# Sample tokens' hi and lo parts as one 128-column stationary operand in a streaming encoder layer

## The chip, the cores and the metric

The kernel runs on one core of a Trainium2 chip. The metric is the device time of one execution in microseconds (us), here the median of three runs. A profiled execution gives a trace of every instruction on TensorE (matmul, PE; its weight loads, PEld), VectorE (DVE), ScalarE (ACT), GpSimd (POOL) and SyncE (SP), and of every DMA.

## What is computed

One step of a one-layer streaming encoder on 2048 prompt tokens and 64 sample tokens, 1024 channels, all in 32-bit floats. Both groups of tokens go through the same layer with the same weights; only their conditioning vectors, their convolution history and their attention keys differ.

```
h  = rms_norm(x) * (1 + sc1) + sh1
z  = h @ w_in                      # conv pair | q | k | v | two gates
u  = glu_a * sigmoid(glu_b)        # causal depthwise conv, LayerNorm, swish, projection
o  = band_attention(q, k, v)       # own chunk of 64 and 8 chunks before, per-head bias
m  = sigmoid(g_conv) * conv_out + sigmoid(g_attn) * attn_out
x  = x + gt1 * (m @ w_o)
h2 = rms_norm(x) * (1 + sc2) + sh2
x  = x + gt2 * ((silu(gate) * up) @ w_ffn_out)   # gate, up = h2 @ w_ffn_in, 2816 each
```

Outputs are the two results and the new convolution, key and value states.

## The kernel before, in words

**Three passes per product.** Each operand of a large product is kept as two parts in a matmul format: hi, a copy that ScalarE makes (`split`, L706), and lo, what is left, which VectorE or POOL subtracts. A product is the sum of three passes (`mm3`, L700): hi x hi, hi x lo and lo x hi; lo x lo is left out. Each pass is one LDWEIGHTS of the stationary operand and one MATMUL that streams the other one, up to 512 columns.

**Two forms.** In *column form* the weights are stationary and tokens stream (convolution pair, gates, merge, FFN up). In *row form* a tile of tokens is stationary, up to 128 of them as columns, and 512 weight columns stream; the result has tokens on the partitions of a PSUM bank. Row form serves q, k and v (`qkv`, L1168, and `first_block`, L899), the output projection (`wo`, L1836) and the FFN's down products (`add_down`, L2136; later blocks also `down_pair` and `add_last`).

**Token tiles.** `token_tiles` (L65) makes the 64 sample tokens a tile of their own, ahead of 128-token prompt tiles. So only the first token block of each phase, tokens 0 to 575 (`PBLOCKS`, `CBLOCKS`), has a sample tile, and in row form its stationary operand has 64 columns.

**Order of the work.** The first phase goes through four token blocks: q, two convolution channels, k, one more step of convolution, v, and so on, gates, with attention and convolution taps let in between. The second phase goes through three blocks: merge, output projection with residual and norm, turn into columns, FFN. What is let in between is decided while the program is written: `Stream` (L170) keeps an estimated clock for each engine, every instruction adds its estimated time, and the lanes (`norm_lane`, `work`, `attn`, `conv`, `tail`, `turns`) issue their next step when TensorE's clock has come far enough. `spend` (L207) ticks that clock after each `mm3`. Weights come from memory through staging tiles, are split by ScalarE and VectorE or POOL (`Weights.split`, L451), and are freed as products are done.

**Places that the change touches.** `turn` (L926) makes the columns of the first block from transposes: VectorE scales them, ScalarE writes `hh`, VectorE writes `hl`. `product` in `first_block` (L955) and in `qkv` (L1173) runs the passes for q, k and v; `qk_rows` and `v_rows` take the finished bank. `merge` (L1677) writes the merged columns as `m[0]` (hi) and `m[1]` (lo). `residual` (L1710) multiplies the projection's banks by the gate, adds x, norms, and transposes. `hidden` (L1900) writes the FFN's hidden columns to `hid` as hi and lo, in two halves of 288 tokens in the first block. `add_down` adds a pair of hidden rows' products for each token tile to an accumulator `acc`; the first pair is copied there by ScalarE, later ones are added by VectorE, and the last group goes through gate and residual to the output. PSUM has four banks (`gp`) for these products in the second phase, two per token tile.

Of the kernel before, what the change touches and what calls it, by code (L numbers as in the profile page):

```python
# [8 lines left out]
F32 = mybir.dt.float32  # L9
# [7 lines left out]
P = 128  # L17
# [594 lines left out]
def streaming_layer(ctx: ExitStack, tc: tile.TileContext, I, O):  # L612
# [87 lines left out]
    def mm3(ps, lh, ll, rh, rl, first, last, **kw):  # L700
# [2 lines left out]
        pe.matmul(ps, ll, rh, start=False, stop=last, **kw)  # L703
        stream.spend()

    def split(hi, lo, src):  # L706
        act.activation(hi, src, AF.Copy)
        stream.after("dve", "act")
        dve.tensor_tensor(lo, src, hi.bitcast(F32), ALU.subtract)
# [49 lines left out]
    def temp(name, shape=(P, 512)):  # L759
        return wk.tile(list(shape), F32, tag="t", name=name, bufs=NT)  # L760
# [138 lines left out]
    def first_block(xs):  # L899

        tiles = token_tiles(*PBLOCKS[0])
        vectors, taps, begun = setup()
        taps = taps()

        def scale_rows(a, b):
            for x_t, (t, n) in list(zip(xs, tiles))[a:b]:
                r = square(x_t, n)
                dve.tensor_scalar(x_t[:n], x_t[:n], r, None, ALU.mult)

        def modulation(ct):  # L910
# [12 lines left out]

            return rest

        def turn(k):  # L926
            pt = ps_a.tile([P, 2, 512], F32, tag="s", name="pt")
            for i, (t, n) in enumerate(tiles):
                o = pt[:, 0, t : t + n] if i < 4 else pt[:, 1, :n]
                pe.transpose(o, xs[i][:n, k * P : (k + 1) * P], ident[:n, :n])  # L930
            h = wk.tile([P, QB + SMP], F32, tag="pr", name="h32", bufs=8)
            for a, e, o, w in ((0, SMP, pt[:, 0, :SMP], 1), (SMP, 448, pt[:, 0, SMP:448], 0), (448, 576, pt[:, 1, :P], 0)):
                dve.tensor_scalar(h[:, a:e], o, A1[:, k, w : w + 1], B1[:, k, w : w + 1], ALU.mult, ALU.add)

            for c in (slice(0, 448), slice(448, 576)) if not k else (slice(0, 576),):
                split(hh[:, k, c], hl[:, k, c], h[:, c])


        with tc.issue_after(begun[0]), tc.issue_after(begun[1]):
            scale_rows(0, 2)  # L940
            rest = modulation(0)
            vectors()
            rest()
            sums_turned = pe.last.ins
            with tc.issue_after(dve.last.ins):
                scale_rows(2, 5)
            with tc.issue_after(act.last.ins), tc.issue_after(dve.last.ins):
                W.reach = W.held
                W.fill()
        with tc.issue_after(sums_turned):  # L950
            turn(0)
        pss = [ps_g.tile([P, 512], F32, tag="gp", name="ps") for _ in tiles]
        ws = {}

        def product(i, k):  # L955
            t, n = tiles[i]
            if k // 2 not in ws:
                ws[k // 2] = W.get(("qkv", 0, k // 2))
            wh, wl = ws[k // 2]
            mm3(pss[i][:n], hh[:, k, t : t + n], hl[:, k, t : t + n], wh[:, k % 2], wl[:, k % 2], k == 0, k == KT - 1)  # L960
            if i == len(tiles) - 1 and k % 2:
                W.done()

        for k in range(KT - 2):
            if k == 2:
                with tc.issue_after(act.last.ins):
                    next(taps)
            turn(k + 1)
            if k and k % 2 == 0:
                rest = modulation(k + 2)  # L970
            for i in range(len(tiles)):
                if i == 2 and not k:
# [167 lines left out]
    def norm_tile(lo, t, free):  # L1140

        c = slice(t - lo, t - lo + P)
        while t not in ahead_x:
            load_ahead()
        x_t, landed = ahead_x.pop(t)
        yield landed
        r = square(x_t, P)
        yield stream.when("pool")
        dve.tensor_scalar(x_t, x_t, r, None, ALU.mult)
        yield stream.when("dve") + PE_LAG  # L1150
        for g in range(2):
# [12 lines left out]
            f = slice(4 * g, 4 * g + 4)  # L1164
            act.activation(hh[:, f, c], h, AF.Copy)
            yield stream.when("act")
            dve.tensor_tensor(hl[:, f, c], h, hh[:, f, c].bitcast(F32), ALU.subtract)
    def qkv(b, m, norms):  # L1168
        lo, hi = PBLOCKS[b]
        tiles = token_tiles(lo, hi)  # L1170
# [2 lines left out]
        def product(t, n, ps, k):  # L1173
            if k // 2 not in ws:
                ws[k // 2] = W.get(("qkv", m, k // 2))
            wh, wl = ws[k // 2]
            c = slice(t - lo, t - lo + n)
            mm3(ps[:n], hh[:, k, c], hl[:, k, c], wh[:, k % 2], wl[:, k % 2], k == 0, k == KT - 1)
            if (t, n) == tiles[-1] and k % 2:
                W.done()  # L1180

        for t, n in tiles:
# [2 lines left out]
            ps = ps_g.tile([P, 512], F32, tag="gp", name="ps")  # L1185
            for k in range(KT):
                product(t, n, ps, k)
            if m == 0:
                work.start(qk_rows(ps, n, gqk[:, 0:1], q_d, t, None))
            elif m == 1:  # L1190
# [485 lines left out]

    def merge(c0, c1, src, m, ahead, load):  # L1677
        n = c1 - c0
        for ct in range(KT):
            g = ahead.pop(0)  # L1680
            if ct == 2 and load:
# [28 lines left out]
    def residual(pp, t, n, gt1, a, half, hs, free, last, i):  # L1710
# [91 lines left out]
    for s, (lo, hi) in enumerate(CBLOCKS):  # L1802
# [4 lines left out]
        for i, (c0, c1) in enumerate(chunks):  # L1807
# [28 lines left out]
            def wo(i, k):  # L1836
# [2 lines left out]
                    ws[k] = W.get(("wo", k))  # L1839
                wh, wl = ws[k]  # L1840
                c = slice(t - c0, t - c0 + n)
                for j in range(2):
                    f = slice(512 * j, 512 * j + 512)
                    mm3(pp[j][:n], m[0][:, k, c], m[1][:, k, c], wh[:, 0, f], wl[:, 0, f], k == 0, k == KT - 1)
                if i == len(grp) - 1:
                    W.done()

# [50 lines left out]
            return hid[i][:, f % 2]  # L1898

        def hidden(f, i, ps):  # L1900
            hi, lo = (hid_of(f)[:, j, i * half : (i + 1) * half] for j in range(2))
            stream.after("act", "dve")
            split(hi, lo, ps)

        class Operands:

# [229 lines left out]
        def add_down(fs, ws):  # L2136

            last = fs[-1] == NF - 1
            for i, (t, n) in enumerate(tiles):
# [6 lines left out]
                for e, j in [(e, j) for e in fs for j in range(2)] if last and not i else [(e, j) for j in range(2) for e in fs]:  # L2146
                    h = hid_of(e)
                    f = slice(512 * j, 512 * j + 512)
                    w = ws[e - fs[0]]
                    mm3(pss[j][:n], h[:, 0, c], h[:, 1, c], w[0][:, 0, f], w[1][:, 0, f], e == fs[0], e == fs[-1])  # L2150
                for j, ps in enumerate(pss):
                    f = slice(512 * j, 512 * j + 512)
                    dst = acc[i][:n, f]
                    stream.after("dve", "pe")
                    if fs[0] == 0:
                        act.activation(dst, ps[:n], AF.Copy)
                    elif not last:
                        dve.tensor_tensor(dst, dst, ps[:n], ALU.add)
# [96 lines left out]
```

## Time and profile before

| | |
|---|---|
| median of 3 runs | 2991.47 us (2991.17 to 2992.53) |
| profiled execution, first to last instruction (span) | 2988.4 us |
| median less span | 3.1 us |
| mean granted TensorE clock | 0.993 |
| TensorE busy | 97% of the span, 16259 matmuls |
| weight loads busy | 87% |
| VectorE, ScalarE, POOL busy | 68%, 45%, 38% |
| moved by DMA | 628 MB, 210 GB/s |

The profile gives of its own execution the span alone; what lies around it is taken as the 3.1 us by which the median of the runs is longer. Busy times of TensorE overlap, since a matmul starts while the one before it drains; the distance between starts is the better measure of a pass. In a row of groups stand the engine, the operation, output and inputs by name, the shape (stationary rows * columns, then the streamed shape), the count, then busy time and the mean length of one in ns, then idle time before them and what ended it.

### The profile page before, as it was taken

To read this page: it belongs to the slowest core of one execution; us is meant where nothing else is said; L and a number is where in the kernel's file an instruction comes from. 1 tells how busy PE (TensorE), PEld (TensorE's weight loads), DVE (VectorE), ACT (ScalarE), POOL (GpSimd) and SP (SyncE) were. 2 spreads that over 40 slices of the span, in tenths; PEclk is the share of its full clock that TensorE was granted. 3 is DMA by queue.
4 is the path that set the end of the run, shared out by engine and by line. 5 is a ranking of instruction groups with operands and counts; after the bars stand their busy time and mean duration, and the time that the engine had idled before them with its cause. 6 is when DMAs were issued, how large, how long until landed. Compare 5 with 4: busy or idle time off the path is not lost. (4 is left out here: it accounts for less than half of the span.)

```text
span 2988.4 us, 44911 instructions
## 1 busy us (share of the span) xinstructions
PE 2911.8 (97%) x16259; PEld 2594.0 (87%) x16259; DVE 2025.1 (68%) x3596; ACT 1355.2 (45%) x2437; POOL 1140.8 (38%) x734
## 2 busy tenths in 40 slices
PE   7999899999999999989999999999999999999999
PEld 4899777787888788878989899999999999999998
DVE  5897687668857885477777755666666657466666
ACT  3345643661465257464444335534444345344442
POOL 0201310111011102444666443255766741465667
PEclk9999999999999999999999999999999999999999
DMA  9989889978987888885444786323333975233333
GB/s 307 305 289 299 271 288 304 280 254 276 304 272 222 278 253 277 267 280 167 139 148 151 231 266 223 132 90 113 113 106 115 307 245 183 95 96 115 115 103 127
DMA packets 467725, 628.06 MB, mean 210 GB/s; under 512 B 36277, under 2 KB 314665, under 8 KB 467502
## 3 DMA queue, kind: packets, MB, share of 16 engines
q1 hardware_dynamic: 453456, 605.58, 62.7%
q10 hardware_dynamic: 14045, 19.60, 1.9%
q8 instruction: 128, 2.10, 0.3%
q14 instruction: 96, 0.78, 0.1%
HBM read 476.53 MB, written 148.54 MB: 209 GB/s over the span
## 5 line engine op out<-in xcount | busy, mean ns | idle before, releaser
L102 PE MATMUL ps<-t,whi 128*128 128x384 f32 (+1 forms) x2112 | 502.6, 322 | 10.3 <-ACT t L102 4.9
L102 POOL TENSOR_TENSOR wlo<-wst,whi 128x1024 fp32r<-128x1024 f32 (+1 forms) x157 | 357.8, 2289 | 288.6 <-ACT whi L102 256.3
L102 ACT ACTIVATE whi<-wst 128x1024 fp32r<-128x1024 f32 (+1 forms) x264 | 257.4, 977 | 335.6 <-PE ps L102 115.9
L102 PE MATMUL ps<-b,whi 128*128 128x384 f32 (+1 forms) x1584 | 381.4, 326 | 6.1 <-DVE early L102 3.3
L102 PEld LDWEIGHTS ps<-t,whi 128*128 128x128 f32 x2112 | 367.5, 188 | 17.8 <-ACT t L102 5.1
L102 DVE SCALAR_TENSOR_TENSOR y<-u,wd,y 128x512 f32<-128x512 f32 (+1 forms) x480 | 369.1, 773 | 6.3
L102 PE MATMUL ps<-hh,whi 128*128 128x512 f32 (+2 forms) x992 | 361.6, 365 | 0.0
L102 DVE TENSOR_TENSOR acc<-acc,pd 128x512 f32<-128x512 f32 (+1 forms) x464 | 311.6, 685 | 67.5 <-PE pd L102 64.8
L102 PE MATMUL ps<-hl,whi 128*128 128x512 f32 (+2 forms) x992 | 345.6, 348 | 0.0
L102 PE MATMUL ps<-hh,wlo 128*128 128x512 f32 (+2 forms) x992 | 345.1, 348 | 0.0
L102 PE MATMUL ps<-t,wlo 128*128 128x384 f32 (+1 forms) x1056 | 339.3, 321 | 1.0 <-POOL wlo L102 0.7
L102 PE MATMUL pd<-whi,hid 128*128 128x512 f32 (+1 forms) x1016 | 325.0, 391 | 0.0
L102 PEld LDWEIGHTS ps<-b,whi 128*128 128x128 f32 x1584 | 278.5, 189 | 12.0 <-DVE early L102 4.2
L102 POOL TENSOR_TENSOR r<-t,mhalf 128x1 f32<-128x1 f32 (+3 forms) x68 | 83.6, 1231 | 455.8 <-DVE t L102 450.6
L102 PE MATMUL ps<-b,wlo 128*128 128x384 f32 (+1 forms) x792 | 256.9, 325 | 0.0
L102 ACT ACTIVATE pr<-pr,sm 128x640 f32<-128x640 f32 (+3 forms) x272 | 200.2, 747 | 109.0 <-DVE sm L102 106.3
L102 PEld LDWEIGHTS pd<-whi,hid 128*128 128x128 f32 (+1 forms) x1016 | 185.9, 183 | 44.5 <-ACT hid L102 0.7
L102 PEld LDWEIGHTS ps<-hh,wlo 128*128 128x128 f32 x992 | 186.7, 188 | 21.8
L102 PEld LDWEIGHTS ps<-hh,whi 128*128 128x128 f32 x992 | 187.2, 189 | 18.6 <-issue 1.6
L102 PEld LDWEIGHTS ps<-hl,whi 128*128 128x128 f32 x992 | 187.5, 189 | 15.6 <-issue 1.4
L102 PEld LDWEIGHTS ps<-t,wlo 128*128 128x128 f32 x1056 | 198.2, 188 | 2.5 <-POOL wlo L102 1.3
L102 PE MATMUL pd<-wlo,hid 128*128 128x512 f32 (+1 forms) x508 | 198.4, 391 | 0.0
(225 smaller groups left out, 6174.2 us busy)
## 6 DMA issues: line engine op xcount, KB each, us to landing
whi<-w_din_h SPq DMA_DIRECT2D x72, 512.0 KB, 6.9
wlo<-w_din_l SPq DMA_DIRECT2D x72, 512.0 KB, 8.5
wst<-sum_d SPq DMA_DIRECT2D x132, 256.0 KB, 2.7
wfo<-in_w_ffn_out SPq DMA_DIRECT2D x64, 512.0 KB, 3.4
wmod<-in_w_ada SPq DMA_DIRECT2D x46, 512.0 KB, 6.2
sum_d<-ws SPq DMA_DIRECT2D x88, 256.0 KB, 3.2
wst<-in_w_ffn_in SPq DMA_DIRECT2D x84, 256.0 KB, 3.1
wst<-in_w_in SPq DMA_DIRECT2D x40, 512.0 KB, 8.5
```

Source lines behind the costliest of these rows:

```text
L102: self.last = f(*args, **kw)
```

## The change

For the sample tile the hi and the lo part stand side by side as one stationary operand of 128 columns, lo in columns 0 to 63 and hi in columns 64 to 127. Two passes, with the weights' hi and then lo part streaming, put the lo rows' product on partitions 0 to 63 of the bank and the hi rows' on 64 to 127 (`mm2`). Afterwards `fold` copies the upper half of the bank to a tile on ScalarE and adds it to the lower half on VectorE. The product lo x lo, left out before, is now part of the sum.

For q, k and v a new tile `both` (in the buffers of tag `vv`, which the attention's values use later) is filled by POOL with copies of the sample columns of `hl` and `hh`. For the output projection and the down products of the first block, `merge` and `hidden` write the parts where they belong: hi is moved up by 64 columns, and the sample's lo columns go in front of it, by a subtraction of their own. The accumulators of `add_down` hold all 128 partitions, and the fold comes once, in the last group. Column-form products, prompt tiles and the later FFN blocks keep three passes.

```diff
+    def mm2(ps, both, rh, rl, first, last, **kw):
+        pe.matmul(ps, both, rh, start=first, stop=False, **kw)
+        pe.matmul(ps, both, rl, start=False, stop=last, **kw)
+        stream.spend()
+
+    def fold(ps, t):
+        stream.after("act", "pe")
+        act.activation(t, ps[SMP : 2 * SMP], AF.Copy)
+        stream.after("dve", "act")
+        dve.tensor_tensor(ps[:SMP], ps[:SMP], t, ALU.add)
...
@@ turn @@
+            for j, x in enumerate((hl, hh)):
+                stream.after("pool", "dve")
+                gps.tensor_copy(both[:, k, SMP * j : SMP * j + SMP], x[:, k, :SMP].bitcast(F32))
...
@@ first_block and qkv @@
+            if t < SMP:
+                fold(pss[i], temp("fold")[:n])
             work.start(qk_rows(pss[i], n, gqk[:, 0:1], q_d, t, None, i > 2))
...
+    both = wk.tile([P, KT, P], F32R, tag="vv", name="both", bufs=2)
+
+    def rows_product(ps, t, n, k, wh, wl, lo):
+        c = slice(t - lo, t - lo + n)
+        if t < SMP:
+            mm2(ps, both[:, k], wh, wl, k == 0, k == KT - 1)
+        else:
+            mm3(ps[:n], hh[:, k, c], hl[:, k, c], wh, wl, k == 0, k == KT - 1)
...
@@ merge (cut is SMP for the chunk with the sample tokens, else 0) @@
-            split(m[0][:, ct, :n], m[1][:, ct, :n], ps[1])
+            hi = m[0][:, ct, cut : cut + n]
+            act.activation(hi, ps[1], AF.Copy)
+            stream.after("dve", "act")
+            if cut:
+                dve.tensor_tensor(m[0][:, ct, :cut], ps[1][:, :cut], hi[:, :cut].bitcast(F32), ALU.subtract)
+            dve.tensor_tensor(m[1][:, ct, cut:n], ps[1][:, cut:], hi[:, cut:].bitcast(F32), ALU.subtract)
...
@@ residual @@
+            if t < SMP:
+                fold(pp[j], x1[:n, f])
             stream.after("dve", "pe")
             dve.tensor_tensor(pp[j][:n], pp[j][:n], gt1[which][:n, f], ALU.mult)
...
@@ wo @@
+                    if t < SMP:
+                        mm2(pp[j], m[0][:, k, : 2 * SMP], wh[:, 0, f], wl[:, 0, f], k == 0, k == KT - 1)
+                    else:
+                        mm3(pp[j][:n], a[:, c], m[1][:, k, c], wh[:, 0, f], wl[:, 0, f], k == 0, k == KT - 1)
...
@@ hidden, first block only @@
+            hi = h[:, 0, SMP:][:, c]
+            act.activation(hi, ps, AF.Copy)
+            stream.after("dve", "act")
+            cut = 0 if i else SMP
+            if cut:
+                dve.tensor_tensor(h[:, 0, :cut], ps[:, :cut], hi[:, :cut].bitcast(F32), ALU.subtract)
+            dve.tensor_tensor(h[:, 1, c][:, cut:], ps[:, cut:], hi[:, cut:].bitcast(F32), ALU.subtract)
...
@@ add_down @@
+                    if t < SMP:
+                        mm2(pss[j], h[:, 0, : 2 * SMP], w[0][:, 0, f], w[1][:, 0, f], e == fs[0], e == fs[-1])
...
-                    dst = acc[i][:n, f]
+                    dst = acc[i][:, f]
...
-                        dve.tensor_tensor(ps[:n], ps[:n], dst, ALU.add)
+                        dve.tensor_tensor(ps, ps, dst, ALU.add)
+                        dst = dst[:n]
+                        if t < SMP:
+                            fold(ps, dst)
                         dve.tensor_tensor(ps[:n], ps[:n], gt[:n, f], ALU.mult)
```

More of the change, by code (lines that the diff above doesn't have):

```diff
@@ L959, in product @@
             wh, wl = ws[k // 2]
-            mm3(pss[i][:n], hh[:, k, t : t + n], hl[:, k, t : t + n], wh[:, k % 2], wl[:, k % 2], k == 0, k == KT - 1)
+            rows_product(pss[i], t, n, k, wh[:, k % 2], wl[:, k % 2], 0)
             if i == len(tiles) - 1 and k % 2:
@@ L1176, in product @@
             wh, wl = ws[k // 2]
-            c = slice(t - lo, t - lo + n)
-            mm3(ps[:n], hh[:, k, c], hl[:, k, c], wh[:, k % 2], wl[:, k % 2], k == 0, k == KT - 1)
+            rows_product(ps, t, n, k, wh[:, k % 2], wl[:, k % 2], lo)
             if (t, n) == tiles[-1] and k % 2:
@@ L1187, in qkv @@
                 product(t, n, ps, k)
+            if t < SMP:
+                fold(ps, temp("fold")[:n])
             if m == 0:
@@ L1678, in merge @@
         n = c1 - c0
+        cut = 0 if c0 else SMP
         for ct in range(KT):
@@ L1841, in wo @@
                 c = slice(t - c0, t - c0 + n)
+                a = m[0][:, k, 0 if c0 else SMP :]
                 for j in range(2):
                     f = slice(512 * j, 512 * j + 512)
-                    mm3(pp[j][:n], m[0][:, k, c], m[1][:, k, c], wh[:, 0, f], wl[:, 0, f], k == 0, k == KT - 1)
+                    if t < SMP:
+                        mm2(pp[j], m[0][:, k, : 2 * SMP], wh[:, 0, f], wl[:, 0, f], k == 0, k == KT - 1)
+                    else:
+                        mm3(pp[j][:n], a[:, c], m[1][:, k, c], wh[:, 0, f], wl[:, 0, f], k == 0, k == KT - 1)
                 if i == len(grp) - 1:
@@ L1900, in hidden @@
         def hidden(f, i, ps):
-            hi, lo = (hid_of(f)[:, j, i * half : (i + 1) * half] for j in range(2))
+            h = hid_of(f)
+            c = slice(i * half, (i + 1) * half)
             stream.after("act", "dve")
-            split(hi, lo, ps)
+            if s:
+                split(h[:, 0, c], h[:, 1, c], ps)
+                return
+            hi = h[:, 0, SMP:][:, c]
[5 more added lines that the diff above has]
+            dve.tensor_tensor(h[:, 1, c][:, cut:], ps[:, cut:], hi[:, cut:].bitcast(F32), ALU.subtract)
         class Operands:
@@ L2149, in add_down @@
                     w = ws[e - fs[0]]
-                    mm3(pss[j][:n], h[:, 0, c], h[:, 1, c], w[0][:, 0, f], w[1][:, 0, f], e == fs[0], e == fs[-1])
+                    if t < SMP:
+                        mm2(pss[j], h[:, 0, : 2 * SMP], w[0][:, 0, f], w[1][:, 0, f], e == fs[0], e == fs[-1])
+                    else:
+                        a = h[:, 0, 0 if s else SMP :]
+                        mm3(pss[j][:n], a[:, c], h[:, 1, c], w[0][:, 0, f], w[1][:, 0, f], e == fs[0], e == fs[-1])
                 for j, ps in enumerate(pss):
                     f = slice(512 * j, 512 * j + 512)
-                    dst = acc[i][:n, f]
+                    dst = acc[i][:, f]
                     stream.after("dve", "pe")
                     if fs[0] == 0:
-                        act.activation(dst, ps[:n], AF.Copy)
+                        act.activation(dst, ps, AF.Copy)
                     elif not last:
-                        dve.tensor_tensor(dst, dst, ps[:n], ALU.add)
+                        dve.tensor_tensor(dst, dst, ps, ALU.add)
                     else:
-                        dve.tensor_tensor(ps[:n], ps[:n], dst, ALU.add)
+                        dve.tensor_tensor(ps, ps, dst, ALU.add)
+                        dst = dst[:n]
+                        if t < SMP:
+                            fold(ps, dst)
                         dve.tensor_tensor(ps[:n], ps[:n], gt[:n, f], ALU.mult)
```

## The prediction

> **What bounds the kernel now.** I read the page first, then busy time by stage, then TensorE's groups by shape, then the chain that ended last, then TensorE's waits.
>
> ```profile
> span 2988.4 us, 44911 instructions
> PE 2911.8 (97%) x16259; PEld 2594.0 (87%) x16259; DVE 2025.1 (68%) x3596; ACT 1355.2 (45%) x2437; POOL 1140.8 (38%) x734
> ```
>
> TensorE is busy for 97% of the span. The same by stage (columns: the stretch, its length, busy time of PE, PEld, DVE, ACT, POOL, granted clock, DMA share, GB/s):
>
> ```profile
> 31.00:75.00 44.00, 42.43 (x283) 30.20 (x283) 26.84 (x54) 13.78 (x21) 2.17 (x2) 1.00 0.97 325
> 75.00:345.00 270.00, 260.41 (x1712) 236.68 (x1710) 212.91 (x401) 130.46 (x273) 54.27 (x48) 1.00 0.88 294
> 1195.00:1300.00 105.00, 104.21 (x621) 92.25 (x621) 56.65 (x115) 50.84 (x83) 50.04 (x24) 0.99 0.84 262
> 1300.00:1345.00 45.00, 34.64 (x213) 31.76 (x212) 34.72 (x60) 26.69 (x54) 21.46 (x18) 0.92 0.85 299
> 1345.00:1755.00 410.00, 405.51 (x2511) 369.02 (x2510) 289.75 (x437) 162.57 (x316) 230.01 (x143) 1.00 0.56 181
> 1755.00:2988.00 1233.00, 1224.94 (x6407) 1137.92 (x6406) 761.30 (x1263) 541.40 (x895) 673.09 (x398) 1.00 0.45 144
> ```
>
> The stretches are: the q product of the first token block; the rest of that block; merge and output projection of the first FFN block; its turn into columns; its FFN; the two later FFN blocks. TensorE idles 1.6, 9.6, 0.8, 10.4, 4.5 and 8.1 us in them. So it is the bound nearly everywhere that sample tokens pass, and what ends after 1345 us follows it almost one to one. VectorE is next, and never full.
>
> A busy TensorE need not be at its peak, so the price of one pass is taken from the distance between starts. The chain that ended last, in the first FFN block (start, length, what, count):
>
> ```profile
> 1522.33 11.23 PE ps L102 x83
> 1533.56 13.66 PE pd L102 x60
> 1547.22 6.20 PE ps L102 x47
> ```
>
> The 60 `pd` passes are one pair of down products: 5 token tiles x 2 rows of weights x 2 column halves x 3 passes, 12 of them the sample tile's. 13.66 / 60 = **0.2277 us per pass**. Sample passes alone, in the output projection:
>
> ```profile
> 1242.68 0.39 PE L102 MATMUL pw<-wlo,m 128*64 128x512 f32 x1
> ...
> 1246.12 0.40 PE L102 MATMUL pw<-wlo,m 128*64 128x512 f32 x1
> ...
> 1252.80 0.71 PE L102 MATMUL pt<-ident,xn 64*128 64x64 f32 x8
> ```
>
> Fifteen passes lie between the two `wlo` starts: 3.44 / 15 = 0.229 us. A pass with 64 stationary columns costs what one with 128 does; half of the array is unused in it.
>
> **The change part by part.** All sample passes in row form:
>
> ```profile
> L102 PE MATMUL pd<-whi,hid 128*64 128x512 f32 x88 | 29.2, 394 | 0.0
> L102 PE MATMUL ps<-whi,hh 128*64 128x512 f32 x24 | 10.5, 436 | 0.2 <-ACT hh L102 0.2
> L102 PE MATMUL pd<-wlo,hid 128*64 128x512 f32 x44 | 17.2, 391 | 0.0
> L102 PE MATMUL pw<-whi,m 128*64 128x512 f32 x32 | 10.7, 391 | 0.0
> L102 PE MATMUL ps<-wlo,hh 128*64 128x512 f32 x24 | 9.7, 406 | 0.0
> L102 PE MATMUL ps<-whi,hl 128*64 128x512 f32 x24 | 9.7, 406 | 0.0
> L102 PE MATMUL pw<-wlo,m 128*64 128x512 f32 x16 | 6.3, 393 | 0.0
> ```
>
> Down: 88 + 44 = 132. Output projection: 32 + 16 = 48. q, k, v: 24 + 24 + 24 = 72. Together 252, of which a third goes: **44 + 16 + 24 = 84 passes**. At 0.2277 us that is 10.0 + 3.6 + 5.5 = **19.1 us** (of the 5.5, q has 1.8, k and v 3.6).
>
> The 168 passes that stay load 128 columns instead of 64:
>
> ```profile
> L102 PEld LDWEIGHTS pd<-whi,hid 128*128 128x128 f32 x928 | 174.1, 188 | 36.9 <-ACT hid L102 0.7
> L102 PEld LDWEIGHTS pd<-whi,hid 128*64 128x64 f32 x88 | 11.7, 134 | 7.6 <-DVE hid L102 0.3
> ```
>
> The load grows from 134 to 188 ns but stays under the 228 ns of the pass beside it, and 128-column passes already start every 0.2277 us. I cost it at nothing; uncovered it would be 168 x 54 ns = 9.1 us. The Trainium skill ("TensorE: Matmul & The Clock Gate", LDWEIGHTS and Back-to-back issue gap) speaks against the change here: a load takes a time that grows with its columns, and loads and passes together set the spacing. By its rule of columns over 1.2 the load would grow by an estimated 53 ns, which these rows confirm (54); that it sets the spacing at 512 moving columns they do not.
>
> What the folds and new pieces cost has these nearest rows:
>
> ```profile
> L102 ACT ACTIVATE other<-po 64x512 f32<-64x512 f32 x32 | 19.0, 593 | 55.0 <-PE po L102 54.7
> L102 DVE TENSOR_TENSOR o_p<-other,po 64x512 f32<-64x512 f32 x32 | 21.9, 683 | 20.8 <-ACT other L102 20.3
> L102 POOL COPY u<-hist 128x30 f32<-128x30 f32 x16 | 4.5, 291 | 33.4 <-DVE hist L102 12.5 <-DVE y L102 11.8 <-DVE sm L102 9.1
> L102 DVE TENSOR_TENSOR hid<-ps,hid 128x288 fp32r<-128x288 f32 x44 | 20.0, 454 | 15.5 <-ACT hid L102 15.4
> L102 DVE TENSOR_TENSOR pl<-ptp,ph 128x256 fp32r<-128x256 f32 x8 | 3.3, 417 | 0.5 <-ACT ph L102 0.5
> L102 DVE TENSOR_TENSOR pl<-ptp,ph 64x64 fp32r<-64x64 f32 x8 | 1.7, 211 | 0.7 <-ACT ph L102 0.7
> L102 DVE TENSOR_TENSOR m<-ps,m 128x320 fp32r<-128x320 f32 x8 | 3.9, 490 | 2.7 <-ACT m L102 2.6
> L102 DVE TENSOR_TENSOR acc<-acc,pd 128x512 f32<-128x512 f32 x448 | 301.9, 685 | 67.5 <-PE pd L102 64.8
> L102 DVE TENSOR_TENSOR acc<-acc,pd 64x512 f32<-64x512 f32 x16 | 10.1, 670 | 0.0
> ```
>
> *Folds.* Seven: one each in q, k and v, two in the output projection, two at the last down products. Each is the pair that attention's end runs already: 0.593 us on ScalarE, then 0.683 us on VectorE, 1.28 us in series, 9.0 us for all if nothing covered them. A fold holds VectorE until ScalarE has copied; behind it wait the tile's own eviction, convolution taps and weight splits, and, for bank or operand, TensorE. In k and v the next token tile gives 24 passes, 5.5 us, of cover. At the last down products the sample's two halves leave about 2.6 us later, and their banks are wanted again only after the next tile's 5.5 us. In the output projection the sample's transposes run at 1252.80 us, 6.7 us after its last `wlo` pass; later ones lie beside the second tile's passes and the second merge. But VectorE is tight in the turn that follows (34.7 of 45 us). I take 1.0 us for the projection's two folds and 0.9 us for the other five, between 0 and 9.0.
>
> *Copies in the first block.* Sixteen copies of 128x64 on POOL; the nearest row has 128x30 at 0.291 us, so about 0.3 each. POOL works for 2.2 us between 31 and 75 us, so they start as soon as the lo part is there, 0.6 us a step. In seven of the eight steps the next step's four full tiles (12 passes, 2.7 us) cover that; in the first nothing does. I take 0.6 us, between 0 and 8 x 0.6 = 4.8.
>
> *Split subtractions.* A 288-column lo part becomes 64 and 224 columns: 0.21 + about 0.39 (just under the 256-column row) for 0.454, 0.15 more, 22 times in the FFN; 0.21 + 0.417 for 0.490 in the eight merges. That is 3.3 + 1.1 us of VectorE beside the 290 of 410 us in which it works there: nothing on the path. Uncovered it would be 4.4 us. *Wider accumulators*: 0.685 for 0.670 us, nothing. The change moves no DMA and adds none; queues keep their contents.
>
> *Where TensorE gets ahead.* In the first block it waits for others, and time gained before such a wait is partly handed back there:
>
> ```profile
> PE pt L102 <- DVE x_t L102: 11.8, 7, 5.6
> PE sc L102 <- DVE sm L102: 8.4, 7, 2.3
> PE ps L102 <- ACT t L102: 4.9, 1, 4.9
> ```
>
> (line, waited for, total, times, longest.) The longest `x_t` wait, 5.6 us, ends a wait of VectorE for POOL in the first block. I let a third of k's and v's 3.6 us go, 1.2, between 0 and 3.6. The `t` wait lies at the turn; its chain starts with TensorE's own last projection pass and moves along with it.
>
> **Sum:** 19.1 - 0.6 - 1.0 - 0.9 - 1.2 = **15.4 us**. The profiled span is 2988.4 us, the median of the runs 2991.5; the 3.1 us around the span stay. Span 2973.0, time **2976 us**.
>
> **The rivals.** *Only the FFN pays.* Everything won before 1300 us is lost at the first block's waits and in the turn; the down products' 10.0 us stay, since TensorE idles for 1% of that stretch: 2981.5. For it: the first block's 9.6 us and the turn's 10.4 us of idleness. Against it: most of those waits follow TensorE's own passes.
>
> *Stalls dealt anew.* The kernel's order is written out by a clock that counts each sample pass; 84 fewer shift when weights are split, taps issued and heads started. The first block's waits may then fall elsewhere and grow. A long one costs twice:
>
> ```profile
> 325.00:350.00 25.00, 17.46 (x87) 13.27 (x85) 11.20 (x33) 14.42 (x35) 8.03 (x7) 0.96 0.96 314
> 350.00:375.00 25.00, 24.88 (x116) 19.58 (x115) 20.96 (x46) 13.22 (x25) 8.30 (x4) 0.90 0.77 245
> ```
>
> The stretch with 7.5 us of TensorE idle, most of it the 5.6 us wait, is followed by one in which the granted clock is 0.90 over 25 us, so about 2.5 us more. The Trainium skill ("TensorE: Matmul & The Clock Gate", The HAM clock gate) says that about 3.4 us of idleness halve the clock until TensorE has been busy as long; this row agrees. One more such wait is 8 us, one and a half 12: 2984 to 2988, say 2987. One fewer gives 2968.
>
> *Loads set the spacing.* The 9.1 us above: 2985. Against it stand the 128-column passes at 0.2277 us.
>
> *Slower.* A fold stops VectorE while ScalarE works off what is queued ahead of the copy. Were that two or three weight splits of about a microsecond each at all seven folds, VectorE would stand for 7 x (3 + 0.7) = 26 us; where TensorE waits for VectorE all the while, 19 us are won and 26 lost: 2998. It decides from a queue of 2 us on. Against it: VectorE has slack in every stretch above, and ScalarE is busy for less than half of all but the turn.
>
> **How the numbers follow.** Chances: the forecast 0.60; only the FFN 0.11; stalls dealt anew for the worse 0.14, for the better 0.07; loads 0.02; slower 0.06. A measurement tells 0.2%, 6 us, from no change. Faster by more than that: 0.60 + 0.11 + 0.07 + 0.02 = 0.80; within it 0.14; slower 0.06. The range reaches down to all 19.1 us and one wait fewer, less a little (2966), and up to the stalls dealt anew (2988).
>
> **What would show it.** Right: 84 fewer matmuls; no 64-column row-form pass left; `pd` pieces of 56 passes in about 12.75 us, still 0.228 each; the stretch of the first FFN block's FFN about 10 us shorter; TensorE's idle time as before. Wrong: a spacing above 0.23 us; a new TensorE wait for `both`, `hid` or a fold; VectorE rows of folds with long idle time before them; more clock lost between 75 and 1345 us.

## The result and the profile after

The changed kernel takes **2997.04 us** (median of 13 runs, 2991.4 to 3000.63) against 2991.3 us for the kernel before beside it (13 runs, 2988.79 to 2995.74): a ratio of **1.0015**, 95% interval 1.0007 to 1.0023. The forecast was 2976 with a range up to 2988. The profiled execution spans 2992.9 us, 4.5 more than that of before, at a mean granted clock of 0.989 for 0.993.

First the page of the changed kernel, then a pair of down products in its chain that ended last (start, length, what, count), then two of TensorE's groups by shape:

```profile
span 2992.9 us, 44792 instructions
PE 2904.1 (97%) x16175; PEld 2597.3 (87%) x16175; DVE 2031.1 (68%) x3640; ACT 1357.6 (45%) x2444; POOL 1132.8 (38%) x743
```

```profile
1402.46 12.73 PE pd L102 x56
```

```profile
L102 PE MATMUL pd<-whi,hid 128*128 128x512 f32 x972 | 314.9, 391 | 0.0
L102 PE MATMUL ps<-whi,both 128*128 128x512 f32 x24 | 10.6, 444 | 0.0
```

16259 - 16175 = 84 matmuls are gone. A pair of down products is 56 passes in 12.73 us, 0.2273 us each, as the 128-column passes of before. The 88 passes with 64 columns have become 44 with 128 (928 + 44 = 972). The work that was to go has gone, at the price that was forecast; the time has been lost elsewhere. To see where, follow the start of the same pass in both traces: the first pass of the first merge, the first FFN up pass, and the first pass of the second block's merge. Before:

```profile
1194.41 0.80 PE L102 MATMUL ps<-cin,whi 128*128 128x320 f32 x2 [1.40 <-DVE o_p L102]
1306.00 0.43 PE L102 MATMUL ps<-b,whi 128*128 128x288 f32 x2
1724.97 0.52 PE L102 MATMUL ps<-cin,whi 128*128 128x384 f32 x2
```

After:

```profile
1213.09 0.56 PE L102 MATMUL ps<-cin,whi 128*128 128x320 f32 x2 [1.40 <-DVE o_p L102]
1320.05 0.43 PE L102 MATMUL ps<-b,whi 128*128 128x288 f32 x2
1728.01 0.52 PE L102 MATMUL ps<-cin,whi 128*128 128x384 f32 x2
```

The second phase begins **18.7 us late**, is 14.1 late at the FFN and 3.0 late behind it. So it wins 4.6 + 11.0 = 15.6 us, and the first phase loses 18.7. Two earlier points split that loss: the first pass of the first convolution channel (behind q) and the one with which the last two channels begin (behind k and v). Before, then after:

```profile
73.70 0.40 PE L102 MATMUL ps<-hh,whi 128*128 128x288 f32 x1
...
172.93 0.29 PE L102 MATMUL ps<-hh,whi 128*128 128x288 f32 x1
```

```profile
74.46 0.40 PE L102 MATMUL ps<-hh,whi 128*128 128x288 f32 x1
...
169.98 0.29 PE L102 MATMUL ps<-hh,whi 128*128 128x288 f32 x1
```

q ends 0.8 us late and gains nothing. Between the two points 2.95 + 0.76 = 3.7 us are won: k's and v's 16 passes at 0.2277 us are 3.6. But for the sample passes both traces hold the same passes between these points, 578 in all before and 562 after. The loss of some 21 us comes after that, in a part whose products are what they were. Stages of before, then of after (columns as in the prediction):

```profile
180.00:345.00 165.00, 155.88 (x1090) 145.76 (x1090) 122.94 (x268) 95.30 (x220) 34.10 (x31) 1.00 0.89 293
345.00:600.00 255.00, 242.20 (x1275) 194.94 (x1276) 190.01 (x380) 115.91 (x226) 31.10 (x27) 0.98 0.90 288
```

```profile
180.00:345.00 165.00, 153.26 (x1044) 142.99 (x1042) 124.91 (x258) 86.88 (x205) 22.84 (x27) 0.96 0.87 287
345.00:600.00 255.00, 235.50 (x1194) 185.38 (x1195) 189.05 (x375) 111.08 (x219) 36.54 (x32) 0.95 0.84 272
```

TensorE is idle for 31.2 us in these 420 us, where it was 21.9: 9.3 more, 6.7 of them behind 345 us. The granted clock is lower by 0.04 over 165 us and 0.03 over 255, together 14 us of full clock, of which what falls under a wait costs nothing. The 21 us lie within the sum of the two, 23. What TensorE waits for between 180 and 600 us (total, times, longest) has changed places. Before:

```profile
PE pt L102 <- DVE x_t L102: 8.8, 4, 5.6
PE sc L102 <- DVE sm L102: 7.7, 6, 2.3
PE pm L102 <- POOL s L102: 3.9, 3, 1.9
```

After:

```profile
PE pm L102 <- POOL s L102: 10.8, 3, 4.4
PE sc L102 <- DVE sm L102: 6.0, 6, 1.7
PE ptp L102 <- ACT pr L102: 5.3, 8, 1.3
```

`pm` is the convolution's column sum: POOL adds the four channels of `y` to `s`, TensorE multiplies `s` with ones, for the LayerNorm's mean and then its variance (`conv_norm`). These are its three waits after:

```profile
279.36 0.69 PE L102 MATMUL pm<-s,ones 128*128 128x64 f32 x2 [4.38 <-POOL s L102]
...
346.79 1.13 PE L102 MATMUL pm<-s,ones 128*128 128x512 f32 x2 [3.21 <-POOL s L102]
...
564.56 2.08 PE L102 MATMUL pm<-s,ones 128*128 128x512 f32 x2 [3.21 <-POOL s L102]
```

And this is what VectorE and POOL do ahead of the first of them:

```profile
272.59 1.73 DVE L102 SCALAR_TENSOR_TENSOR y<-u,wd,y 128x606 f32<-128x606 f32 x2
274.23 1.22 DVE L102 TENSOR_TENSOR wlo<-wst,whi 128x1024 fp32r<-128x1024 f32 x1
...
275.37 3.50 DVE L102 SCALAR_TENSOR_TENSOR y<-u,wd,y 128x606 f32<-128x606 f32 x4
...
279.01 0.29 POOL L102 TENSOR_TENSOR s<-s,y 128x64 f32<-128x64 f32 x1 [34.06 <-DVE y L102]
```

An idle time of POOL of 34 us ends with the last convolution tap, VectorE runs taps and a weight split without a gap, and `pm` was put into TensorE's queue for a moment at which the planner took the taps to be done. What stands behind `pm` in that queue comes after it: TensorE is idle for 4.4 us. A stretch with such a wait is paid a second time, by the granted clock. The 25 us around the third one, in before and in after:

```profile
550.00:575.00 25.00, 24.26 (x125) 19.95 (x125) 15.54 (x33) 19.15 (x33) 8.28 (x7) 1.00 0.81 244
```

```profile
550.00:575.00 25.00, 20.11 (x90) 16.01 (x89) 20.16 (x38) 11.87 (x23) 4.74 (x5) 0.86 0.81 265
```

TensorE is idle for 4.9 us where it was 0.7, and 0.86 for 1.00 over 25 us is 3.5 us of clock on top. This is the rival that the prediction named "stalls dealt anew", twice as dear as it was priced.

### The profile page after: what moved, and what is told of

It is laid out like the page before. It is cut to its first block, busy times and chain, and to the rows that moved or that the text cites. A ratio compares the mean times of both kernels' runs of the same rounds, so it can differ in the third digit from the quotient of the medians.

```text
span 2992.9 us, 44792 instructions
## 1 busy us (share of the span) xinstructions
PE 2904.1 (97%) x16175; PEld 2597.3 (87%) x16175; DVE 2031.1 (68%) x3640; ACT 1357.6 (45%) x2444; POOL 1132.8 (38%) x743
## 4 chain that ended last, share of the span: by engine, by line
PE 81%; DVE 9%; DMA 4%; ACT 2%; issue 2%; POOL 1%; SPq 0%; ACTq 0%; DVEq 0%; POOLq 0%
PE ps L102 53%; PE pd L102 15%; PE pw L102 5%; DVE y L102 3%; PE po L102 2%; PE sc L102 2%; PE ptp L102 2%; DVE wlo L102 1%; PE pt L102 1%; ACT whi L102 1%; PE pa L102 1%; DMA tg<-g_d 1%; POOL r L102 1%; DVE pw L102 1%; DVE pr L102 1%
## 5 line engine op out<-in xcount | busy, mean ns | idle before, releaser
L102 DVE TENSOR_TENSOR acc<-acc,pd 128x512 f32<-128x512 f32 x464 | 311.9, 685 | 63.6 <-PE pd L102 61.0
L102 PE MATMUL pd<-whi,hid 128*128 128x512 f32 x972 | 314.9, 391 | 0.0
L102 PEld LDWEIGHTS pd<-whi,hid 128*128 128x128 f32 x972 | 182.6, 188 | 37.3 <-ACT hid L102 0.7
L102 PEld LDWEIGHTS ps<-hl,whi 128*128 128x128 f32 x992 | 188.6, 190 | 15.6 <-issue 1.6
L102 PE MATMUL pd<-wlo,hid 128*128 128x512 f32 x508 | 198.7, 391 | 0.0
```

The lines of the kernel that those rows point to most:

```text
L102: self.last = f(*args, **kw)
```

## The experiments

**The theory**: the change's work is worth what was forecast; what loses time is the order of the instructions, planned from an estimated clock that now counts 84 passes fewer (and the folds and copies more). **The rival**: the new work itself (folds, copies, the q product's waits) disturbs the first phase. In the expectations A is the first, B the second, and A1 to A3 ask which part of the new clock does it: two passes counted in q, k and v (A1), folds and copies counted (A2), or any shift at all (A3). Each kernel was timed beside runs of before on the same chip; "late" is the start of the first merge against the 1194.41 us of before's profile, and "pm" TensorE's wait for `s` between 180 and 600 us.

| kernel | median us | ratio to before, 95% interval | late us | pm us |
|---|---|---|---|---|
| the change | 2997.04 | 1.0015 (1.0007 to 1.0023) | 18.7 | 10.8 |
| e1 change, order of before | 2982.72 | 0.9969 (0.9956 to 0.9981) | 5.2 | 3.3 |
| e2 before, order of the change | 3011.96 | 1.0064 (1.0050 to 1.0078) | 24.1 | 10.5 |
| e3 second phase only | 2980.23 | 0.9963 (0.9950 to 0.9975) | 6.0 | 3.9 |
| e4 third pass counted in q, k, v | 2984.18 | 0.9975 (0.9964 to 0.9986) | 11.0 | 4.5 |
| e5 folds, copies uncounted | 2995.54 | 1.0009 (1.0000 to 1.0018) | 18.4 | 4.1 |
| e6 before, clock 2 us ahead | 2995.10 | 1.0007 (0.9998 to 1.0016) | 5.8 | 2.0 |
| e7 before, clock 2 us behind | 2996.57 | 1.0009 (1.0000 to 1.0019) | 7.8 | 2.5 |
| e9 third pass counted in q | 2996.51 | 1.0014 (1.0005 to 1.0023) | 20.9 | 10.9 |
| e10 counted in k and v | 2979.17 | 0.9956 (0.9942 to 0.9970) | -0.8 | 2.0 |
| e11 q as before, k, v counted | 2983.27 | 0.9969 (0.9957 to 0.9980) | 10.4 | 5.4 |
| e12 counted in k | 2987.38 | 0.9986 (0.9977 to 0.9994) | 10.3 | 4.3 |
| e13 counted in v | 2981.72 | 0.9972 (0.9963 to 0.9982) | 5.9 | 7.5 |
| e14 the change, pm 4 us later | 2983.05 | 0.9964 (0.9951 to 0.9978) | 7.9 | 1.0 |
| e15 before, pm 4 us later | 2993.90 | 0.9999 (0.9990 to 1.0009) | 0.1 | 1.3 |
| e16 e10, pm 4 us later | 2979.29 | 0.9951 (0.9939 to 0.9964) | -2.3 | 1.3 |

One caution for the columns from profiles: they are of one execution. e3 has the first phase of before and is 6.0 us late in its profile; its median does not show that. Differences of a few us in them mean nothing.

### Order and work taken apart

**e1** keeps all of the change and plans it with the clock of before: a third pass is counted, folds, copies and the split pieces are issued without counting.

```diff
 def mm2(ps, both, rh, rl, first, last, **kw):
     pe.matmul(ps, both, rh, start=first, stop=False, **kw)
     pe.matmul(ps, both, rl, start=False, stop=last, **kw)
+    stream.add("pe", "matmul", ps.shape[1], (ps, both), kw)
     stream.spend()
 def fold(ps, t):
-    stream.after("act", "pe")
-    act.activation(t, ps[SMP : 2 * SMP], AF.Copy)
+    nc.scalar.activation(t, ps[SMP : 2 * SMP], AF.Copy)
...
```

> All of the change, but the planner's clock runs as before: each sample product still counts three passes, folds, copies and split pieces count nothing. The order of issue is that of the kernel before but for the new instructions. Theory A (the shifted clock dealt the first phase a new order, and its waits are what was lost): the 84 passes come off, 2991.3 - 15 to 19 = 2972 to 2976, and TensorE's starts in the first phase lie within 6 us of those before. Rival B (the folds and the copies themselves hold VectorE and POOL up, whatever the order): the loss stays, 2994 to 3000, with the first phase some 20 us late at the first merge.

**e2** is its mirror image, the kernel before with its three passes, planned with the clock of the change.

```diff
 # mm3
+        if ps.shape[0] == SMP:
+            stream.load["pe"] -= 512 / 2.4
 # after each sample product, where the change folds
+    stream.after("act", "pe")
+    stream.add("act", "activation", 512, (), {})
+    stream.after("dve", "act")
+    stream.add("dve", "tensor_tensor", 512, (), {})
...
```

> The kernel before, three passes and no fold, but with the planner's clock of the change: sample products count two passes, folds and copies and split pieces count as if they were there. The order of issue is that of the change. Theory A: before plus what the order costs, about 24 us in the first phase, less nothing: 3010 to 3018. Rival B: no fold and no copy, so no loss: 2988 to 2995.

e2 removes no work and adds none, and takes 3011.96 us, 20.4 more than the 2991.61 beside it. It has the change's waits, and this is its first merge:

```profile
PE pm L102 <- POOL s L102: 10.5, 3, 4.4
```

```profile
1218.53 0.56 PE L102 MATMUL ps<-cin,whi 128*128 128x320 f32 x2 [1.40 <-DVE o_p L102]
```

It is 24.1 us late. So with the work of before the change's order alone costs some 20 us, and it costs them before the second phase. e1 gains 8.9 us where e2 loses 20.4, so A stands and B falls; but e1 misses its 2972 to 2976. It has a wait of its own in the first block:

```profile
PE pt L102 <- DVE kn L102: 4.3, 1, 4.3
```

The same wait is 0.2 us before. Here the folds aren't counted, so k's transposes stand in TensorE's queue ahead of the moment at which their rows are ready: an order planned for other work need not suit this one. The 4.3 us are a part of the 7 to 11 us by which e1 misses; the rest is not explained.

Whether e1 and e2 have the orders that they stand for can be read from the traces. TensorE's passes of the first phase, in order of start and named by output and inputs, without the sample passes of q, k and v, are 6439 in every kernel. Two such lists are compared line by line, and the lines without a partner are counted on both sides. Before and e1 differ in 68 lines, the change and e2 in 108, but before and the change in 1216; before and e3 (next) are equal. Read crosswise by medians, the order costs 20.4 us with the old work and 14.3 with the new (e1 to the change), and the work is worth 8.9 us in the order of before and 14.9 in that of the change (e2 to the change).

**e3** leaves q, k and v alone and makes the change in the second phase only.

```diff
-        if t < SMP:
-            mm2(ps, both[:, k], wh, wl, k == 0, k == KT - 1)
-        else:
-            mm3(ps[:n], hh[:, k, c], hl[:, k, c], wh, wl, k == 0, k == KT - 1)
+        mm3(ps[:n], hh[:, k, c], hl[:, k, c], wh, wl, k == 0, k == KT - 1)
```

> The change in the output projection and the down products alone; q, k and v keep three passes, no copies and no folds there, so the first phase is issued as before. 60 passes go, 13.7 us. Theory A and rival B alike: the first phase as before, 2991.3 - 10 to 14 = 2977 to 2981. If it is slower than that, the second phase does not pay as priced; if it is at 2991 or above, the loss is not in q, k and v at all.

2980.23: 11.4 us faster, inside its range. The second phase's gain is real and reaches the end. All profiles bear it out, whatever the order: from the first merge to the second block's merge it is 529 to 533 us in the five kernels with the old work (before, e2, e6, e7, e15) and 514 to 520 in the twelve others.

### Which part of the clock

**e4** counts the third pass in q, k and v and also the folds and copies; **e5** counts two passes, but not the folds and copies of q, k and v.

```diff
 # e4, mm2 as called by rows_product
+        if third:
+            stream.add("pe", "matmul", ps.shape[1], (ps, both), kw)
 # e5, fold in q, k, v and the copies to both
-                stream.after("pool", "dve")
-                gps.tensor_copy(both[...], x[...])
+                nc.gpsimd.tensor_copy(both[...], x[...])
```

> All of the change; only in q, k and v the planner's clock still counts a third pass for each sample product, while folds and copies count. Theory A1 (it is the clock running short by the missing passes that dealt the bad order): 2977 to 2984, like the run with the old clock. Theory A2 (it is the folds and copies that it counts): 2993 to 3000, like the change. Theory A3 (any shift deals the first phase anew, and neither is the cause by itself): a third place, more than 4 us from both.

> All of the change; only in q, k and v the folds and the copies count nothing in the planner's clock, while the sample products count their two passes. Theory A1: 2993 to 3000. Theory A2: 2977 to 2984. Theory A3: a third place, more than 4 us from both.

2984.18, at the upper end of A1's range, and 2995.54, inside it: A1. The passes that aren't counted any more make the bad order; counting folds or not changes little.

**e6** and **e7** shift TensorE's clock of the kernel before once, behind the first block's v, by 2 us.

```diff
+        if b == 0 and stage == "v":
+            stream.load["pe"] += 2000.0   # e7: -= 2000.0
```

> The kernel before, no work changed; TensorE's planner clock is set 2 us ahead once, after the first block's v product. Theory A3: the first phase is dealt anew and the time leaves 2991.3 by 4 us or more, to either side; most likely upwards, 2995 to 3010. Theories A1 and A2 say nothing of it; if it stays within 2988 to 2995, the first phase bears such shifts and the order of the change is a bad one by its own content.

> The kernel before, no work changed; TensorE's planner clock is set 2 us back once, after the first block's v product, in the direction of the change. Theory A3: 2991.3 left by 4 us or more, to either side. If a shift of that size and sign is what costs the change its gain: 3005 to 3015.

2995.10 and 2996.57, 2.6 and 4.1 us above the 2992.51 beside them. The interval of e6's ratio holds 1 and that of e7's begins there, so it is not shown that either shift costs anything, and neither costs the twenty of the change's order. The 3005 to 3015 of e7's expectation falls; e6 lies on the border between its two answers.

**e9** and **e10** count the third pass in q alone and in k and v alone; **e12** and **e13** in k and in v; **e11** is e10 with q's product as before, and its copies uncounted.

```diff
 # rows_product: q (e9) | k and v (e10) | k (e12) | v (e13)
-            mm2(ps, both[:, k], wh, wl, k == 0, k == KT - 1)
+            mm2(ps, both[:, k], wh, wl, k == 0, k == KT - 1, third)
```

> The change with the third pass counted in TensorE's estimated clock for q only; k and v count two. It tells which product's clock sets the bad order. If k's and v's clock does it (they are followed at once by the attention and convolution steps that are let in): TensorE's order differs from the change's in few places, and the time is the change's, 2993 to 3000. If q's does it (everything after q is planned from an earlier start): 2980 to 2988.

> The mirror image: the third pass counted in TensorE's clock for k and v, q counts two. If k's and v's clock sets the bad order: 2980 to 2988, near the run that counted the third pass in all three products (2984.2). If q's does: 2993 to 3000.

> As the run that counted the third pass in k and v, but in k only (8 passes, 1.7 us of estimated time); v counts two. If the loss follows how far the estimated clock runs short, half the correction gives about half the way: 2986 to 2991. If v's missing time alone sets the bad order: 2993 to 3000; if k's alone does: 2977 to 2983. Three different answers for k and v alone, neither half nor all, would mean that each shift deals the waits anew and has no owner.

> The mirror image: counted in v only, k counts two. If the loss is in proportion to the missing time: 2986 to 2991, as with k. If v's missing time alone sets the bad order: 2977 to 2983; if k's alone: 2993 to 3000. Both this and its mirror image near 2980 would mean that only the change's own combination is bad; both near 2997, that either shift is enough.

> q with its three passes and 64 columns as before, k and v in two passes counted as three, their folds counted, the second phase as in the change. If the 16 passes of k and v are a gain that reaches the end once the order is not the bad one: 3.6 us below the run that changed the second phase alone (2980.2), so 2975 to 2978.5. If the folds' place in the order (it is nearly that of the run that counted the third pass in all three products) or the waits of the first phase take it back: 2980 to 2985.

e9 stays at the change's time, and nearly at its order (152 lines differ); e10 gains 12.9 us on the 2992.11 beside it: the missing time of **k and v** makes the bad order, q's doesn't. Counted from the change's median, k's alone brings back 9.7 us and v's alone 15.3 of the 17.9 that both bring: the shares don't add up, so the loss is not in proportion to the missing time. e11, in spite of winning k's and v's passes, isn't better than e3: it falls into its second case, and its waits for `s` are back at 5.4 us. e10, which differs from the change only in what the planner counts, is better than the kernel before and the change; from e3 it can't be told apart (the intervals overlap). Its first and second merge:

```profile
1193.63 0.56 PE L102 MATMUL ps<-cin,whi 128*128 128x320 f32 x2 [1.40 <-DVE o_p L102]
...
1708.04 0.52 PE L102 MATMUL ps<-cin,whi 128*128 128x384 f32 x2
```

The first merge is on before's time, the second 16.9 us ahead of it. (This profile is e10's shortest run, 2973.59; its median is 2979.17.)

### Is it the column sum

The bad orders have `pm` waits of 10.5 to 10.9 us (the change, e2, e9). **e14** edits that step alone: both column sums are issued 4 us of estimated time later, and what comes behind is planned from there. **e15** and **e16** do the same to the kernel before and to e10.

```diff
 # conv_norm, ahead of each total()
-        yield stream.when("pool") + PE_LAG
+        yield stream.when("pool") + PE_LAG + 4000.0
         pm = total()
```

> The change, with both of the convolution's column sums (pm) issued 4 us of estimated time later behind POOL's sum than they were; nothing else is edited, though the steps behind them move along. If the three waits at pm (10.8 us, and the half clock behind them) carry the loss of the first phase: 2977 to 2985, TensorE's waits for s under 3 us. If they are only where a TensorE that is ahead happens to stop, the time shows up at the next step of the same kind: 2992 to 3000.

> The same edit in the kernel before, where the waits at pm are 3.9 us. If the edit cures what the change's order brought: 2986 to 2993. If later column sums are simply better in any order, the gain is as large as in the change, 2972 to 2980. If any shift of the order costs about what the two shifted clocks did: 2994 to 2998.

> The same edit in the version that counts the third pass in k and v (2979.2), where waits at pm are 2.0 us. If there is nothing left to cure: 2976 to 2982. If the shift deals the waits anew: 2983 to 2990.

e14 takes 2983.05, 14 us less than the change; the two intervals of the ratio lie far apart. Its wait for `s` in the same stretch, and its two merges:

```profile
PE pm L102 <- POOL s L102: 1.0, 1, 1.0
```

```profile
1202.32 0.56 PE L102 MATMUL ps<-cin,whi 128*128 128x320 f32 x2 [1.40 <-DVE o_p L102]
...
1719.02 0.52 PE L102 MATMUL ps<-cin,whi 128*128 128x384 f32 x2
```

The wait for `s` falls from 10.8 to 1.0, TensorE's idle time between 180 and 600 us from 31.2 to 22.8, and the first merge comes 10.8 us sooner. e15 and e16, which had little to cure, stay where before and e10 are (0.9999 for 1, 0.9951 for 0.9956). This fits column sums that carry most of the loss, but it does not show it. The edit deals the first phase anew: e14's order differs from the change's in 1306 lines, e10's in 1198. e13 has 7.5 us of waits at `pm` and gains. And e5, as late as the change and with the same idle time of 31.2 us, has most of it at other steps:

```profile
PE sc L102 <- DVE sm L102: 8.9, 10, 1.7
PE ptp L102 <- ACT pr L102: 5.8, 10, 1.7
PE pm L102 <- POOL s L102: 4.1, 2, 3.6
```

The rival is that the change's order is one bad draw, and that nearly any other is better. The table speaks for it. Ten kernels do all of the change's work. Three of them have its order or one near it (e9 152 lines away, e5 462) and take 2995.5 to 2997.0 us; the other seven (e1, e4, e10, e12, e13, e14, e16), each over 1000 lines away, take 2979 to 2987. So it is shown that this order is a bad one, that leaving out k's and v's third pass leads to it, and where TensorE stands in it; that its waits at `pm` are the cause is not shown.

## Why the prediction was wrong

- **Passes of the down products and the projection: right.** 84 fewer, 0.2273 us each at 128 columns, so loads cost nothing. The FFN's stretch was to win 10.0 and wins 11.0. From the first merge to the FFN 3.6 - 1.0 were forecast and 4.6 won, a difference within what profiles spread: the folds of the projection cost nothing visible. e3 says 11.4 for the whole second phase by medians.
- **k and v: right on the spot.** 3.7 us for 3.6. Of a third lost at later waits there was no sign by itself: the later waits were new ones. That these 3.6 us reach the end is not shown either: at the first merge no kernel is more than 2.3 us ahead of before, and e1 and e11, which have them, are not faster than e3, which hasn't.
- **q: wrong by its whole gain.** 1.8 - 0.6 was forecast, 0.8 lost in the profile. TensorE's idle time between 31 and 75 us grew from 1.6 to 3.4 us, as much as the 8 passes are worth. Its largest wait there, for `R`, the modulation's rows, grew from 1.0 to 2.2 us, and the one ahead of it, for the modulation's weights from memory, from 0.3 to 0.7. That fits a q bound by its loads, and the DMA share of 0.97 in the prediction's row of this stretch could have raised the question; it is not shown. No run isolates it, and the end of q also moves by up to 2.4 us between profiles of kernels whose q is the same.
- **Copies**: forecast 0.3 us each; those of the lo part took 0.24, those of the hi part 0.83 (below). TensorE waited 0.5 us for them in all.
- **Slower by a held VectorE: no.** The fold additions of q, k and v idled VectorE for 1.8 us in all.
- **The step that failed** is "*Where TensorE gets ahead*", with the rival "*Stalls dealt anew*" behind it. The prediction counted an earlier TensorE as a gain that a wait hands back, at most 3.6 us, and gave the new order 0.14 and one more wait, 8 to 12 us. The runs show that the new order alone costs 20.4 us with no work changed (e2) and 14.3 with the change's work (e1 to the change), through more idle time of TensorE and the lower clock beside it, and (e4, e9, e10) that k's and v's uncounted passes make it. The rival's mechanism was named rightly; its size was out by a factor of about two. Whether a chance of 0.14 was too low these runs can't tell: of the orders tried for this work, the change's and its near ones are the only bad ones, and as far as these runs tell it is luck which order a change gets.
- **Where it looked.** Its rows by stage leave out 345 to 1195 us, since no sample tokens pass there; the greater part of the loss lies between 345 and 600 us, 6.7 us of idle time and 7.7 of clock. Its rows of waits are of the whole execution: in the rest of the first block, 75 to 345 us, the waits for `x_t` and `sm` are 3.2 and 1.3 us, and the one of 5.6 us ends at 349 us, behind it.
- **The sum itself** is borne out in part. 15.4 us was forecast; with the order held, the work is worth 8.9 us in that of before (e1) and 14.9 in that of the change (e2 to the change). e10, the best of the orders tried, gives 0.9956 of before's time, 13 us (9 to 17 by its interval). Its second phase is shown by e3; the gain that it counts in the first phase is clear of noise in no run's time.

Open stays why the taps are late in just this order. VectorE's taps in the 20 us up to the end of the first `pm` wait:

```profile
L102 DVE SCALAR_TENSOR_TENSOR y<-u,wd,y 128x606 f32<-128x606 f32 x17 | 14.4, 846 | 0.2
```

The planner counts 75 + 1.04 x 606 = 705 ns for one; 17 of them are 2.4 us more than planned. That fits a `pm` that comes too early, but taps take as long in e3 (842 ns each), whose first phase is that of before, and correcting the planner's constant wasn't tried.

## What to carry to other kernels

Where the order of instructions is computed from estimated times, removing work is two edits: the work and the order. Time them apart (new work with the old clock, old work with the new clock) before judging either, and expect that an order can cost more than a small saving brings. When an order goes bad, look where the bound engine stands for a step that was put ahead of a late producer. Moving that step may help, but a better time doesn't show that the step was the cause, since the rest is planned anew with it. Here each of seven other orders for the same work was 10 to 18 us faster than the change's.

## What the runs showed of the hardware

**Short waits add up to half clock.** The changed kernel's stretches of 5 us around 495 us, and TensorE's idle times of over 0.9 us in them:

```profile
490.00:495.00 5.00, 2.40 (x13) 1.66 (x11) 2.88 (x7) 1.74 (x4) 0.21 (x1) 1.00 1.04 386
495.00:500.00 5.00, 3.19 (x13) 2.70 (x12) 4.83 (x12) 4.14 (x10) 0.00 (x0) 0.53 0.30 89
500.00:505.00 5.00, 4.94 (x20) 2.89 (x20) 4.93 (x8) 2.75 (x5) 0.00 (x0) 0.50 1.03 226
```

```profile
492.42 0.85 PE L102 MATMUL sc<-kk,q 128*128 128x320 f32 x4 [1.68 <-DVE sm L102]
494.20 0.85 PE L102 MATMUL sc<-kk,q 128*128 128x320 f32 x4 [0.92 <-DVE sm L102]
495.98 1.43 PE L102 MATMUL sc<-kk,q 128*128 128x320 f32 x4 [0.93 <-DVE sm L102]
```

No wait is longer than 1.7 us, and over the next ten the granted clock is 0.53 and 0.50. So a wait's price can't be read from its length alone. The Trainium skill ("TensorE: Matmul & The Clock Gate", The HAM clock gate) gives an idle window of about 3.4 us as the trigger; here 1.68, 0.92 and 0.93 us with about 0.85 us of work between them were enough.

**A POOL copy stood until VectorE's subtraction ended.** Sixteen copies of 128x64, in two groups (duration in ns, least, median, most), and the longest of them between VectorE's instructions:

```profile
L102 POOL CAST both<-hh x8: 692/826/2253, 28.0 to 69.5; 128x64 fp32r<-128x64 f32 x8
L102 POOL CAST both<-hl x8: 236/237/274, 28.7 to 70.6; 128x64 fp32r<-128x64 f32 x8
```

```profile
30.38 2.35 DVE L102 TENSOR_TENSOR wlo<-wst,whi 128x1024 fp32r<-128x1024 f32 x2
31.25 2.25 POOL L102 CAST both<-hh 128x64 fp32r<-128x64 f32 x1 [2.31 <-ACT hh L102]
32.65 0.76 DVE L102 TENSOR_TENSOR hl<-h,hh 128x576 fp32r<-128x576 f32 x1
33.47 0.24 POOL L102 CAST both<-hl 128x64 fp32r<-128x64 f32 x1
```

A copy of this size took 0.24 us in the second group; this one starts beside VectorE's subtractions and ends at 33.50 us, just behind the last of them at 33.41. The Trainium skill ("GPSIMD Engine Reference", Specifications) says that POOL shares its memory interface with VectorE and contends with instructions that read two inputs there, as these subtractions do; the rows agree. Here a short POOL copy that the same producer released as a VectorE subtraction took as long as the subtraction, 0.83 us (median) beside 0.76.
